# RWKV scan of a two-block network: bonus add, low parts and zero fills taken off POOL, fewer operand parts per stretch

## Chip, cores and metric

One core of a Trainium2 chip. The metric is the device time in microseconds of one launch, the median of several runs. One further execution was taken with the hardware profiler; all rows below come from it.

## What is computed

The reference runs a first block (two layers of attention, gated linear attention and pooling) and a second block whose stages are an SGU, an RWKV mixer, a latent attention and another SGU. Only the RWKV stage is touched by the change. It has 1024 model channels, 16 heads of 64 and 768 tokens (512 and 256 of context), and scans the tokens in both directions:

```
xs   = h + center_shift(h) * mu                      # six mixes: r, k, v, z, decay, a
rkvz = einsum(xs[:4], w_in)                          # four projections 1024x1024
decay, a = lora(xs[4]), lora(xs[5])                  # low rank, per direction
S    = S * w_t - s_kk x (kk_t * a_t) + v_t x k_t     # state 64x64, per head and direction
y_t  = S r_t
yn   = layernorm_per_head(y) * ln_gain + ln_bias
bonus = sum(r * k_dir * r_k) * v
out  = ((yn + bonus) * silu(z)) @ w_out
```

Everything is float32. Large matmuls are done as three products of high and low parts (x = hi + lo, each rounded for TensorE).

## The kernel before, in words

The RWKV stage is the class `Rwkv`. It has two halves, and in both TensorE's instructions keep the order in which the Python code issues them, while the order on the other engines is set by a scheduler when the program is built. Each engine then works through its own queue in order, POOL (GpSimd) and SP (DMA issue) too.

**Features** (`features`, L1316). `strips` runs the projections k, r, z, v: 32 strips of 48 matmuls, in stretches of 12; 1536 matmuls per side product. In between, side generators get credits per stretch: `lora`, `operands` at the rate `OPS`, `by_tokens` (values transposed to tokens) at 2.5 and `first` at 3.0. `operands` (L1570) makes, for each of eight slices of 128 channels (two heads), what the scan needs, in some 15 parts: low-rank matmuls (L1603) with ACT's tanh (L1604), a head norm (transposes, L1264), then for each direction a running sum on VectorE (L1625), exponentials on ACT, and the products L1619, L1646, L1647 and L1649 on VectorE that fill the tiles `st_ar` and `st_bk`. These go to DRAM, and `within` (L1679) multiplies them in blocks of a chunk of 64 tokens; its results go to DRAM as well (`rw_md`, `rw_mo`). `first` starts when the projection z is done: it runs `inverse` 0 on VectorE and `merge` 0, waits until all eight slices have their operands, opens the scan's pool, and starts `inverse` 1 on POOL and the first products.

**Inverse and merge.** `inverse` (L1802) inverts 96 triangular blocks of 32x32 by 31 pairs of a product (L1819) and a subtraction (L1821), and writes the result to DRAM (L1825, then two DMAs). `merge` loads it into a tile `TT`, fills the upper blocks with zeros (L1846, POOL) and joins two 32x32 inverses into one of 64x64 by small matmuls (L1854, L1866). `TT` is a new tile for each slice.

**Scan** (`scan`, L1689). For p = 0 to 8, `lanes` walks 12 steps of slice p and of slice p − 1, interleaved: a step is a chain of 64x64 matmuls on TensorE (all L1885) and copies between (rh L1892, VU L1897 on ACT and L1898, state L1908, SV L1914 and L1915). `weave` mixes in the products of coming slices, `merge` of slice p + 1, `inverse` of slice p + 2 on POOL, and `output` of slice p − 2. `output` normalizes `yacc` (L1945, ACT's square L1948, L1955), scales it on ACT (L1957), adds the bonus on POOL (L1959), multiplies with z on VectorE (L1961), splits into high and low part (`split`, L174, low part on POOL at L178), and multiplies by w_out, whose low weight parts come from VectorE and every third from POOL (`wtile`, L141).

Of the kernel before, what the change touches and what calls it, by code (L numbers as in the profile page):

```python
# [16 lines left out]
ALU = mybir.AluOpType  # L17
# [334 lines left out]
class Block1:  # L352
# [353 lines left out]
    def gla(self, l, P, ap, tmp, idxT, qb, kb, vb, rb, mix_tile):  # L706
# [21 lines left out]

        def merge(X, Y, mask, first):
            pps = [net.aux() for h in range(4)]  # L730
            for c in range(NCH):
                for h in range(4):
                    nc.tensor.matmul(pps[h][:, c * 128:c * 128 + 128], lhsT=X[h * 32:h * 32 + 32, c * 128:c * 128 + 128],
                                     rhs=Y[h * 32:h * 32 + 32, c * 128:c * 128 + 128], start=True, stop=True,
# [9 lines left out]
        for m in (64, 32, 16, 8, 4, 2, 1):  # L744
# [11 lines left out]
            if m == 64:  # L756
                merge(X, X, self.lev64f, True)
            else:
# [358 lines left out]
CH = 64  # L1117
NS = (S + C) // CH
# [31 lines left out]
def chain(*gens):  # L1150
    for g in gens:
        yield from g
# [29 lines left out]
OW = (0.0, 0.4, 1.0)  # L1182
BANKS = (4, 4)
PACE = 0.4
OPS = 2.4
WT = 3


class Rwkv:
# [32 lines left out]
    def work(self, tag, shape, bufs, k=0):  # L1222

        at = {"T12": 1, "TT": (3, 2, 0)[k % 3]}.get(tag)
        if at is None:
            return (self.op if tag[:3] == "inv" and tag != "invW" else self.ap).tile(shape, F32, tag=tag, name=tag, bufs=bufs)
        return shaped(self.big(at), shape)
# [86 lines left out]
    def features(self):  # L1314
# [22 lines left out]
        with tc.tile_pool(name="rws", reuse_waits="tile", bufs=9) as self.xsp:  # L1337
# [3 lines left out]
            vt = chain(*[self.by_tokens(f) for f in range(KD)])  # L1341
            sides = [(self.lora(), 1.0), (ops, OPS), (vt, 2.5), (self.first(), 3.0)]
            self.sides = ops, vt
# [131 lines left out]
    def first(self):  # L1475

        tc = self.net.tc
        while self.done["xs"] != "v":
            yield
        self.cur = cur = [{} for k in range(KD)]  # L1480
        X = [self.big(2), self.big(3)]
        cut = lambda t, a, n: t[:, a:a + n]
        place = {"invA": [cut(X[0], 0, 1024)], "invT": [cut(X[1], 0, 1024)], "invP": [cut(X[0], 1024, 256)]}
        turn = {}

        def work(tag, shape, bufs, k=0):
            if tag == "T12":
                return self.work(tag, shape, bufs, k)
            turn[tag] = turn.get(tag, -1) + 1
            return shaped(place[tag][turn[tag] % len(place[tag])], shape)  # L1490

        acc = self.net.aux
        for _ in self.inverse(0, cur[0], work, self.net.nc.vector):
            yield
        t = self.big(2)
        place = {"invW": [cut(t, 768, 256), cut(t, 1024, 256)], "TT": [self.big(3)]}
        yield from self.merge(0, cur[0], work, acc)

        while self.done["op"] < KD:
            yield  # L1500
        self.right.close()
        self.op = self.right.enter_context(tc.tile_pool(name="rwc", reuse_waits="tile", bufs=1, side="right"))
        self.masks(self.op.tile([128, 2, 64], F32, name="rmask"))
        self.slot, self.groups, self.gs = 0, 0, []
        self.steps_to_come = self.ahead(cur)
        inv = self.inverse(1, cur[1], self.work, self.net.nc.gpsimd)
        for _ in range(9):
            next(self.steps_to_come)
            for _ in range(2):
                next(inv)  # L1510
                yield
        yield from inv
# [319 lines left out]
    def merge(self, k, cur, work, acc):  # L1832

        net, nc, ap = self.net, self.net.nc, self.ap
        mt = cur["mt"]
        TA = cur["TT"] = work("TT", [128, 2, NS, CH], 1, k)
        T12 = work("T12", [128, 2, 24, 32], 1)
        T1, M = T12[:, 0], T12[:, 1]
        TF = TA.rearrange("p d s t -> p (d s) t")
        for e in range(2):  # L1840
            nc.sync.dma_start(M[64 * e:64 * e + 32], self.mo[k][e])
            nc.sync.dma_start(T1[64 * e:64 * e + 32], self.blocks(mt[1], e, 0))
            for h in range(2):
                q = 64 * e + 32 * h
                nc.sync.dma_start(TF[q:q + 32, :, 32 * h:32 * h + 32], self.blocks(mt[0], e, h))
            nc.gpsimd.memset(TF[64 * e + 32:64 * e + 64, :, 0:32], 0.0)  # L1846
        for _ in range(8):
            yield
        for g in range(3):
            pw = acc()  # L1850
            for x in range(8):
                for e in range(2):
                    a, bq = slice(64 * e, 64 * e + 32), slice(64 * e + 32, 64 * e + 64)
                    nc.tensor.matmul(pw[bq, x * 32:x * 32 + 32], lhsT=M[a, g * 8 + x, :], rhs=T1[a, g * 8 + x, :],  # L1854
                                     start=True, stop=True, tile_position=(64 * e, 64 * e + 32))
            yield
            W = work("invW", [128, 8, 32], 2)
            for e in range(2):
                bq = slice(64 * e + 32, 64 * e + 64)
                nc.scalar.copy(W[bq].rearrange("p a b -> p (a b)"), pw[bq, :256])  # L1860
            yield
            pz = acc()
            for x in range(8):
                for e in range(2):
                    a, bq = slice(64 * e, 64 * e + 32), slice(64 * e + 32, 64 * e + 64)
                    nc.tensor.matmul(pz[a, x * 32:x * 32 + 32], lhsT=W[bq, x, :], rhs=TF[bq, g * 8 + x, 32:64],  # L1866
                                     start=True, stop=True, tile_position=(64 * e + 32, 64 * e))
            yield
            for e in range(2):
                a = slice(64 * e, 64 * e + 32)  # L1870
                nc.scalar.activation(TF[a, g * 8:g * 8 + 8, 32:64], pz[a, :256].rearrange("p (x c) -> p x c", c=32), AF.Copy, scale=-1.0)
            yield
# [60 lines left out]
    def output(self, k, cur):  # L1933

        net, nc, ap, P = self.net, self.net.nc, self.ap, self.P
        T = S + C
        rows = slice(k * 128, k * 128 + 128)
        col = lambda t, j: t[:, j:j + 1]
        y = cur["y"]
# [11 lines left out]
        z, bonus = (ap.tile([128, T], F32, tag="f", name="ld_" + n) for n in "zb")  # L1951
# [4 lines left out]
        yield  # L1956
        nc.scalar.activation(y, y, AF.Identity, scale=col(P["lg"], k), bias=col(P["lb"], k))  # L1957
        yield
        nc.gpsimd.tensor_tensor(y, y, bonus, ALU.add)  # L1959
        yield  # L1960
        nc.vector.scalar_tensor_tensor(y, y, 0.5, z, ALU.mult, ALU.mult)  # L1961
        yield
        yh = ap.tile([128, T], F32R, tag="yh", name="yh", bufs=1)
        yl = ap.tile([128, T], F32R, tag="yl", name="yl", bufs=1)
        net.split(yh, yl, y, nc.gpsimd)
        yield
        for f in range(KD):
            if f % 4 == 0:
                hi, lo = net.wtile([(0, net.I["rwkv_w_out_2"][0][rows, f * 128:f * 128 + 512])], 1, 512)
            a, b = net.acc(), net.acc()  # L1970
            outs = [(a, 0, S), (b[:, :C], S, T)]
            net.strip(outs, [(hi[:, 0], lo[:, 0])], [(yh, yl)], c0=f % 4 * 128)
            yield
            self.b2.residual(self.i, f, outs, ap if k == KD - 1 else None)
# [488 lines left out]
```

## Time and profile before

| | us |
|---|---|
| median of 3 runs | 4227.73 |
| lowest, highest | 4226.45, 4228.69 |
| the profiled execution's own time | 4218.81 |
| its span | 4216.9 |
| RWKV features, about | 2009 to 2532 |
| eight operand slices in them | 2140 to 2393 |
| RWKV scan, about | 2536 to 3072 |

Times in rows are microseconds from the start of the span unless marked ns. PE is TensorE, PEld its weight loads, DVE VectorE, ACT ScalarE, POOL GpSimd, SP the engine that issues DMAs. A releaser ("[1.2 <-ACT tmp L1604]") is what ended the idle time in front of an instruction. PEclk is the clock that TensorE was granted, as a share of full speed.

### The profile page before, as it was taken

The page shows a single profiled execution, that of the slowest core. Times are in us where ns is not written, and L with a number is a line of the kernel's source. Part 1 is how long each engine was busy: PE and PEld are TensorE (multiplying, and loading weights), DVE is VectorE, ACT ScalarE, POOL GpSimd, SP SyncE. Part 2 cuts the span into 40 slices and gives each one's busy share as a digit, 9 for nine tenths or more (in the row PEclk, how much of TensorE's full clock was granted, in tenths as well). Part 3 has the DMA queues.
Part 4 walks back from the last instruction along what each step waited for, and adds up shares of the span by engine and source line. Part 5 has one row for each costly group of instructions (what it writes and reads, how often), then busy time and mean ns, then how long its engine had stood idle before and what let it go on. Part 6 is the DMA issues. An engine that isn't in the chain of part 4 may idle for free. (4 is left out here: it accounts for less than half of the span.)

```text
span 4216.9 us, 67232 instructions
## 1 busy us (share of the span) xinstructions
PE 3855.6 (91%) x26432; PEld 3192.2 (76%) x26432; DVE 2461.7 (58%) x4804; ACT 1545.2 (37%) x2945; POOL 1317.8 (31%) x1340
## 2 busy tenths in 40 slices
PE   8999999999999999998887797588789899998999
PEld 7867777787877788887766576477577788887887
DVE  7836445865554434444767644477643778883544
ACT  4243223334332422223454433244343455553222
POOL 3321111322111211113445578820121344442221
PEclk9999999999999999999899898799889999999999
DMA  3125543213364322222257866355223121221332
GB/s 92 51 79 162 175 132 90 61 56 100 103 202 158 102 65 61 60 61 78 70 158 202 226 166 156 91 128 124 79 61 114 51 61 52 61 77 62 93 91 85
DMA packets 599015, 431.72 MB, mean 102 GB/s; under 512 B 193436, under 2 KB 532140, under 8 KB 598700
## 3 DMA queue, kind: packets, MB, share of 16 engines
q1 hardware_dynamic: 593756, 414.97, 34.1%
q0 software_dynamic: 4944, 12.46, 1.2%
q8 instruction: 209, 3.42, 0.3%
q14 instruction: 106, 0.87, 0.1%
HBM read 354.46 MB, written 68.68 MB: 100 GB/s over the span
## 5 line engine op out<-in xcount | busy, mean ns | idle before, releaser
L138 ACT CAST whi<-wraw 128x1024 fp32r<-128x1024 f32 (+3 forms) x471 | 457.5, 972 | 1183.0 <-PE acc L160 971.4
L141 POOL TENSOR_TENSOR wlo<-wraw,whi 128x1024 fp32r<-128x1024 f32 (+2 forms) x205 | 426.9, 2083 | 1291.3 <-ACT whi L138 1182.1
L160 PE MATMUL acc<-hh,whi 128*128 128x512 f32 (+2 forms) x1776 | 625.2, 377 | 9.5 <-ACT hh L421 5.0
L160 PE MATMUL acc<-hl,whi 128*128 128x512 f32 (+2 forms) x1776 | 620.8, 374 | 2.5 <-DVE hl L422 2.5
L160 PE MATMUL acc<-hh,wlo 128*128 128x512 f32 (+2 forms) x1776 | 620.3, 374 | 2.0 <-DVE wlo L141 2.0
L141 DVE TENSOR_TENSOR wlo<-wraw,whi 128x1024 fp32r<-128x1024 f32 (+3 forms) x266 | 330.6, 1244 | 467.1 <-ACT whi L138 420.7
L160 PEld LDWEIGHTS acc<-hh,whi 128*128 128x128 f32 (+1 forms) x1776 | 314.7, 188 | 84.0 <-ACT whi L138 17.3
L160 PEld LDWEIGHTS acc<-hh,wlo 128*128 128x128 f32 (+1 forms) x1776 | 314.4, 187 | 63.4 <-DVE wlo L141 2.8
L160 PEld LDWEIGHTS acc<-hl,whi 128*128 128x128 f32 (+1 forms) x1776 | 314.6, 188 | 62.3 <-DVE hl L422 4.1
L160 PE MATMUL acc<-wlo,hh 128*128 128x256 f32 (+1 forms) x896 | 297.2, 332 | 6.5 <-DVE wlo L141 6.5
L160 PE MATMUL acc<-whi,hh 128*128 128x256 f32 (+1 forms) x896 | 298.1, 335 | 2.9 <-ACT hh L978 2.3
L160 PE MATMUL acc<-whi,hl 128*128 128x256 f32 (+1 forms) x896 | 293.4, 331 | 1.5 <-DVE hl L979 1.5
L999 DVE SCALAR_TENSOR_TENSOR xT<-acc,mod,xT 128x512 f32<-128x512 f32 x256 | 185.6, 746 | 139.6 <-PE acc L160 138.9
L160 PEld LDWEIGHTS acc<-wlo,hh 128*128 128x128 f32 x896 | 179.5, 201 | 20.4 <-DVE wlo L141 7.3
L160 PEld LDWEIGHTS acc<-whi,hh 128*128 128x128 f32 x896 | 179.4, 201 | 20.5 <-ACT hh L978 2.9
L160 PEld LDWEIGHTS acc<-whi,hl 128*128 128x128 f32 x896 | 178.4, 200 | 16.3 <-DVE hl L979 2.4
L160 PE MATMUL wide<-xsh,whi 128*128 128x512 f32 (+1 forms) x512 | 147.4, 371 | 16.5 <-ACT xsh L1384 16.5
L160 PE MATMUL wide<-xsl,whi 128*128 128x512 f32 (+1 forms) x512 | 142.0, 360 | 17.0 <-POOL xsl L1385 13.5
L160 PE MATMUL wide<-xsh,wlo 128*128 128x512 f32 (+1 forms) x512 | 140.0, 356 | 0.0
L160 PE MATMUL acc<-ffgh,whi 128*128 128x512 f32 x352 | 139.9, 400 | 0.0
L160 PE MATMUL acc<-ffgl,whi 128*128 128x512 f32 x352 | 138.4, 395 | 0.0
L160 PE MATMUL acc<-ffgh,wlo 128*128 128x512 f32 x352 | 138.3, 395 | 0.0
(625 smaller groups left out, 8754.9 us busy)
## 6 DMA issues: line engine op xcount, KB each, us to landing
ada_w<-in_ada_w SPq DMA_DIRECT2D x32, 1536.0 KB
wraw<-in_sgu_w_in SPq DMA_DIRECT2D x96, 512.0 KB
wraw<-in_w_up SPq DMA_DIRECT2D x88, 512.0 KB
wraw<-in_w_in SPq DMA_DIRECT2D x44, 512.0 KB
wraw<-in_w_down SPq DMA_DIRECT2D x32, 512.0 KB
wraw<-in_sgu_w_out SPq DMA_DIRECT2D x32, 512.0 KB
wraw<-in_rwkv_w_in SPq DMA_DIRECT2D x32, 512.0 KB
bk<-rw_bk SPq DMA_DIRECT2D x24, 512.0 KB
```

The source lines that it names most:

```text
L138: nc.scalar.copy(hi, raw)
L141: eng.tensor_tensor(lo, raw, hi.bitcast(F32), ALU.subtract)
L160: mm(out, lhsT=a, rhs=b[:, t0:t1], start=first and n == 0, stop=last and n == 2)
L999: nc.vector.scalar_tensor_tensor(dst[k], ps, m[:, 16 + k, j:j + 1], dst[k], ALU.mult, ALU.add)
```

## The change

Four edits, all in the RWKV stage:

- `OPS`, the parts of `operands` issued per stretch of 12 projection matmuls, goes from 2.4 to 1.7.
- The bonus add (L1959) and the low part of `yacc` (L178) are done by VectorE.
- The low parts of w_out's weights are all done by VectorE.
- The tile `TT` of a merge is allocated for slices 0, 1 and 2 alone and then used in turn, so that its zeros, now written by VectorE, are written for these three only. The other parts of the tile are written anew by every merge.

```diff
@@ -1182,7 +1182,7 @@
 OW = (0.0, 0.4, 1.0)
 BANKS = (4, 4)
 PACE = 0.4
-OPS = 2.4
+OPS = 1.7
 WT = 3
 
 
@@ -1478,6 +1478,7 @@
         while self.done["xs"] != "v":
             yield
         self.cur = cur = [{} for k in range(KD)]
+        self.tts = []
         X = [self.big(2), self.big(3)]
         cut = lambda t, a, n: t[:, a:a + n]
         place = {"invA": [cut(X[0], 0, 1024)], "invT": [cut(X[1], 0, 1024)], "invP": [cut(X[0], 1024, 256)]}
@@ -1833,7 +1834,10 @@
 
         net, nc, ap = self.net, self.net.nc, self.ap
         mt = cur["mt"]
-        TA = cur["TT"] = work("TT", [128, 2, NS, CH], 1, k)
+
+        if k < 3:
+            self.tts.append(work("TT", [128, 2, NS, CH], 1, k))
+        TA = cur["TT"] = self.tts[k % 3]
         T12 = work("T12", [128, 2, 24, 32], 1)
         T1, M = T12[:, 0], T12[:, 1]
         TF = TA.rearrange("p d s t -> p (d s) t")
@@ -1843,7 +1847,8 @@
             for h in range(2):
                 q = 64 * e + 32 * h
                 nc.sync.dma_start(TF[q:q + 32, :, 32 * h:32 * h + 32], self.blocks(mt[0], e, h))
-            nc.gpsimd.memset(TF[64 * e + 32:64 * e + 64, :, 0:32], 0.0)
+            if k < 3:
+                nc.vector.memset(TF[64 * e + 32:64 * e + 64, :, 0:32], 0.0)
         for _ in range(8):
             yield
         for g in range(3):
@@ -1956,17 +1961,17 @@
         yield
         nc.scalar.activation(y, y, AF.Identity, scale=col(P["lg"], k), bias=col(P["lb"], k))
         yield
-        nc.gpsimd.tensor_tensor(y, y, bonus, ALU.add)
+        nc.vector.tensor_tensor(y, y, bonus, ALU.add)
         yield
         nc.vector.scalar_tensor_tensor(y, y, 0.5, z, ALU.mult, ALU.mult)
         yield
         yh = ap.tile([128, T], F32R, tag="yh", name="yh", bufs=1)
         yl = ap.tile([128, T], F32R, tag="yl", name="yl", bufs=1)
-        net.split(yh, yl, y, nc.gpsimd)
+        net.split(yh, yl, y)
         yield
         for f in range(KD):
             if f % 4 == 0:
-                hi, lo = net.wtile([(0, net.I["rwkv_w_out_2"][0][rows, f * 128:f * 128 + 512])], 1, 512)
+                hi, lo = net.wtile([(0, net.I["rwkv_w_out_2"][0][rows, f * 128:f * 128 + 512])], 1, 512, nc_lo=nc.vector)
             a, b = net.acc(), net.acc()
             outs = [(a, 0, S), (b[:, :C], S, T)]
             net.strip(outs, [(hi[:, 0], lo[:, 0])], [(yh, yl)], c0=f % 4 * 128)
```

Line numbers of the changed kernel are higher by one to five in this part of the file (L1679 is L1680, L1885 is L1890, L1959 is L1964).

TensorE in the features, at the second operand slice: the two block products (`st_ar`, `st_bk`) of a slice and the low-rank matmuls and transposes of the next; left out are the projection matmuls between. Before:

```order
L1679 MATMUL aux<-st_ar,st_bk 64x64 x24
...
L1679 MATMUL aux<-st_ar,st_bk 64x64 x24
L1603 MATMUL aux<-hw,w_17814 128x512 x2
L1603 MATMUL aux<-hw,w_17814 128x256 x2
...
L1603 MATMUL aux<-ha,a_17815 128x512 x2
L1603 MATMUL aux<-ha,a_17815 128x256 x2
L1264 MATMUL aux<-ident,hs_rep 128x128 x6
...
L1679 MATMUL aux<-st_ar,st_bk 64x64 x24
```

In the change, at the same slice:

```order
L1680 MATMUL aux<-st_ar,st_bk 64x64 x24
...
L1680 MATMUL aux<-st_ar,st_bk 64x64 x24
...
L1604 MATMUL aux<-hw,w_17891 128x512 x2
L1604 MATMUL aux<-hw,w_17891 128x256 x2
L1604 MATMUL aux<-ha,a_17892 128x512 x2
L1604 MATMUL aux<-ha,a_17892 128x256 x2
L1264 MATMUL aux<-ident,hs_rep 128x128 x6
...
L1680 MATMUL aux<-st_ar,st_bk 64x64 x24
```

Before, the marks "..." stand for 24, 12 and 36 projection matmuls; in the change for 36, 12 and 60. Over all, the eight slices lie between the 444th and the 1080th of the 1536 projection matmuls before, and between the 444th and the 1380th in the change; merge 0 is at the 1356th in both.

VectorE in the last part of the features, during inverse 0 (its two tiles are the xx tiles). Before:

```order
L1821 TENSOR_TENSOR xx_19673<-xx_19673,xx_19672 96x8x24
L1819 TENSOR_TENSOR xx_19672<-xx_19672,xx_19673 96x175
L1821 TENSOR_TENSOR xx_19673<-xx_19673,xx_19672 96x7x25
L1819 TENSOR_TENSOR xx_19672<-xx_19672,xx_19673 96x156
L1565 TENSOR_TENSOR rst<-aux,rst 128x512
```

In the change:

```order
L1820 TENSOR_TENSOR xx_19350<-xx_19350,xx_19351 96x135
L1611 SCALAR_TENSOR_TENSOR kq<-ld_k,col_rwkv,aux 128x512
L1611 SCALAR_TENSOR_TENSOR kq<-ld_k,col_rwkv,aux 128x256
L1822 TENSOR_TENSOR xx_19351<-xx_19351,xx_19350 96x27x5
L1620 SCALAR_TENSOR_TENSOR tmp<-tmp,kq 128x768
L1650 TENSOR_TENSOR st_ar<-eb,kq 128x12x64
L1820 TENSOR_TENSOR xx_19350<-xx_19350,xx_19351 96x156
L1620 SCALAR_TENSOR_TENSOR tmp<-tmp,kq 128x768
L1648 SCALAR_TENSOR_TENSOR st_bk<-tmp 128x12x64
```

The operands of the last slices now stand between the steps of the inverse, which had its place among the projection's work alone.

POOL in the scan before, at output 0: the end of one inverse, the zero fill of a merge, and further down the bonus add in the middle of the next inverse:

```order
L1825 TENSOR_SCALAR invA<-invT 96x1024
L1829 DMA rw_mt<-invT 96x1024
L1819 TENSOR_TENSOR invP<-invA,invT 96x31
L1828 DMA rw_mt<-invA 96x1024
L1821 TENSOR_TENSOR invT<-invT,invP 96x31
L1846 MEMSET xx_22597 32x24x32 x2
...
L1819 TENSOR_TENSOR invP<-invA,invT 96x240
L1959 TENSOR_TENSOR yacc<-yacc,ld_b 128x768
L1821 TENSOR_TENSOR invT<-invT,invP 96x12x20
```

VectorE in the change, at the same output 0:

```order
L1960 TENSOR_TENSOR yacc<-yacc,acc 128x512
L1960 TENSOR_TENSOR yacc<-yacc,acc 128x256
L1903 COPY VU<-aux 64x2x64
L1964 TENSOR_TENSOR yacc<-yacc,ld_b 128x768
L1903 COPY VU<-aux 64x2x64
L1913 SCALAR_TENSOR_TENSOR st<-st,rw_ec,aux 128x64 x2
L1966 SCALAR_TENSOR_TENSOR yacc<-yacc,ld_z 128x768
L1920 TENSOR_TENSOR SV<-st,rw_ec 64x2x64
L1913 SCALAR_TENSOR_TENSOR st<-st,rw_ec,aux 128x64 x2
L1920 TENSOR_TENSOR SV<-st,rw_ec 64x2x64
L178 TENSOR_TENSOR yl<-yacc,yh 128x768
```

The add and the low part (yl) stand among the copies and state updates of the lanes. In POOL's queue of the change the inverses follow one another with no memset of a merge and no operation of an output between.

## Rows read from the trace of the kernel before

**Rows 1.** The page, part 1: busy time, share and instructions of each engine.
```profile
PE 3855.6 (91%) x26432; PEld 3192.2 (76%) x26432; DVE 2461.7 (58%) x4804; ACT 1545.2 (37%) x2945; POOL 1317.8 (31%) x1340
```

**Rows 2.** Stretches: from, to, length, busy (instructions) per engine, PEclk, DMA share, GB/s.
```profile
core 0: us, PE busy (x) PEld busy (x) DVE busy (x) ACT busy (x) POOL busy (x), PEclk, DMA share, GB/s
2140.00:2393.00 253.00, 192.47 (x1572) 154.31 (x1572) 181.70 (x147) 132.82 (x201) 133.35 (x76) 0.91 0.74 202
2393.00:2479.00 86.00, 70.86 (x364) 58.47 (x358) 60.23 (x89) 24.27 (x34) 56.52 (x80) 0.86 0.71 194
...
2650.00:2695.00 45.00, 0.76 (x14) 0.50 (x10) 1.84 (x4) 0.79 (x4) 39.52 (x72) 0.53 0.20 50
2695.00:2710.00 15.00, 14.05 (x162) 11.55 (x162) 9.09 (x30) 3.62 (x11) 13.34 (x24) 0.70 0.03 7
2710.00:3042.00 332.00, 289.31 (x4981) 237.33 (x4976) 241.78 (x765) 130.53 (x400) 71.06 (x93) 0.95 0.48 115
```

**Rows 3.** Timeline of TensorE in the scan: start, duration, operation, [idle before, releaser].
```profile
2695.30 1.12 PE L1885 MATMUL aux<-rh,xx 64*64 64x64 f32 x16 [44.29 <-DVE rh L1892]
```

**Rows 4.** Timeline of VectorE at the same place.
```profile
2693.61 1.43 DVE L1961 SCALAR_TENSOR_TENSOR yacc<-yacc,ld_z 128x768 f32<-128x768 f32 x1 [43.12 <-POOL yacc L1959]
```

**Rows 5.** Timeline of POOL at the same place.
```profile
2691.78 1.80 POOL L1959 TENSOR_TENSOR yacc<-yacc,ld_b 128x768 f32<-128x768 f32 x1
```

**Rows 6.** Timeline of ScalarE, the operation before the bonus add.
```profile
2647.00 1.03 ACT L1957 ACTIVATE yacc<-yacc,col_rwkv 128x768 f32<-128x768 f32 x1 [0.25 <-DVE yacc L1955]
```

**Rows 7.** Waits of POOL, 2535 to 3075: total, times, longest.
```profile
POOL yacc L1959 <- ACT yacc L1957: 131.7, 6, 47.7
POOL xx L1846 <- PE aux L1885: 74.8, 3, 30.4
```

**Rows 8.** Waits of TensorE, 2140 to 2393.
```profile
PE aux L1679 <- DVE st_bk L1647: 40.6, 13, 5.6
PE aux L1264 <- ACT tmp L1604: 15.9, 11, 3.7
PE aux L1603 <- ACT tmp L1604: 4.0, 5, 2.4
```

**Rows 9.** Timeline of TensorE between two slices: projection matmuls and one `within`.
```profile
2319.25 0.51 PE L160 MATMUL wide<-xsl,whi 128*128 128x512 f32 x2
2319.60 0.52 PE L160 MATMUL wide<-xsh,wlo 128*128 128x512 f32 x2
...
2332.88 2.82 PE L1679 MATMUL aux<-st_ar,st_bk 64*64 64x64 f32 x48 [4.57 <-DVE st_bk L1647]
```

**Rows 10.** Groups of VectorE's instructions, 2710 to 3042: busy us, mean ns, idle before.
```profile
L1915 DVE TENSOR_TENSOR SV<-st,rw_ec 64x128 f32<-64x128 f32 x65 | 24.3, 394 | 1.5
...
L1961 DVE SCALAR_TENSOR_TENSOR yacc<-yacc,ld_z 128x768 f32<-128x768 f32 x6 | 5.7, 953 | 4.5 <-POOL yacc L1959 4.5
```

**Rows 11.** Groups of POOL's instructions, 2536 to 3075.
```profile
L1959 POOL TENSOR_TENSOR yacc<-yacc,ld_b 128x768 f32<-128x768 f32 x8 | 14.5, 1809 | 131.7 <-ACT yacc L1957 131.7
```

**Rows 12.** Timeline of VectorE at 2575 us.
```profile
2575.52 1.85 DVE L1915 TENSOR_TENSOR SV<-st,rw_ec 64x128 f32<-64x128 f32 x1
```

**Rows 13.** Timeline of POOL at 2575 us.
```profile
2575.29 1.94 POOL L1825 TENSOR_SCALAR invA<-invT 96x1024 f32<-96x1024 f32 x1
```

**Rows 14.** Groups of VectorE's instructions, 2140 to 2393: first and last of five.
```profile
L1625 DVE TENSOR_TENSOR_SCAN tmp<-rreset,tmp 128x768 f32<-128x768 bf16 x16 | 28.8, 1843 | 34.8 <-ACT tmp L1621 34.8
...
L1646 DVE TENSOR_TENSOR st_ar<-eb,ld_r 128x768 f32<-128x768 f32 x16 | 22.0, 1373 | 11.4 <-PE aux L1679 5.0 <-DMA ld_r<-rw_r 4.0 <-ACT kd L1617 1.2
```

**Rows 15.** Groups of VectorE's instructions, 2390 to 2540: inverse 0.
```profile
L1821 DVE TENSOR_TENSOR xx<-xx,xx 96x31 f32<-96x31 f32 (+15 forms) x31 | 17.9, 578 | 1.0
L1819 DVE TENSOR_TENSOR xx<-xx,xx 96x31 f32<-96x31 f32 (+15 forms) x31 | 17.4, 563 | 1.0
```

**Rows 16.** Timeline of POOL: the first product of inverse 1.
```profile
2413.47 0.62 POOL L1819 TENSOR_TENSOR invP<-invA,invT 96x31 f32<-96x31 f32 x1
```

**Rows 17.** Line L1825, the end of an inverse, 2400 to 2800: min/median/max ns, first and last start.
```profile
L1825 POOL TENSOR_SCALAR invA<-invT x7: 1912/1944/2059, 2480.9 to 2751.7; 96x1024 f32<-96x1024 f32 x7
```

**Rows 18.** Line L1854, a merge's matmuls in the scan, 2400 to 2800.
```profile
L1854 PE MATMUL acc<-xx x384: 191/191/257, 2571.3 to 2785.2; 32*32 32x32 f32 x192
```

## The prediction

> **What bounds the kernel now.** I read the page's busy shares first, then the stretches of the RWKV stage, then in each stretch the wait that ends last. TensorE is busy 91% of the span and no other engine passes 58% [rows 1], so time can come only from places where TensorE stands still or runs at its lower clock. Only the RWKV stage (about 2009 to 3072 us) is touched. Two stretches of it stand out [rows 2]. From 2650 to 2695 TensorE is busy 0.76 us of 45, and in the 15 us behind that its granted clock is 0.70. From 2140 to 2393, where the eight operand slices run among the projection matmuls, it is busy 192.5 of 253 us, so 60.5 us stand still. Behind these the projections' last part (2393 to 2479) shows 15 us of standing still, and the rest of the scan (2710 to 3042) 43 us of 332.
>
> The long hole has one cause. TensorE waits 44.29 us for VectorE's rh copy [rows 3]; VectorE waited 43.12 us in front of its L1961 [rows 4] for POOL's bonus add L1959, which started at 2691.78 [rows 5]. What that add needs had been there since 2648.03: ACT's L1957 began at 2647.00 and took 1.03 us [rows 6]. So the add stood 43.7 us in POOL's program order behind inverse work. POOL's order shows it: from the memsets (L1846) on nearly a whole inverse stands between them and the add. POOL's other waits are of the same make: 74.8 us in front of the memsets for TensorE's readers and 131.7 us in front of the bonus adds for ACT [rows 7]. Since POOL serves scan operations and inverses in one queue, each of the two holds the other up.
>
> In the operands the waits are TensorE's: 40.6 us at `within` (L1679) for VectorE's st_bk, 15.9 and 4.0 us for ACT's tanh [rows 8], together all of the 60.5. They are the latency of one slice's chain, ACT to VectorE to TensorE, and they appear where few projection matmuls stand between two links: the L1679 at 2332.88 waited 4.57 us [rows 9] with 24 of them ahead of it.
>
> **The change, part by part.**
>
> *Bonus add, low part and memsets leave POOL.* The hole of 44.3 us goes. What is late next there is ACT's L1957 and two VectorE operations, all done within some 4 us of 2648, where the lanes have other work: I take −44.3. Bounds: −44.3, and −20 if a second wait of half the length forms. The clock behind the hole comes back as well: 14.05 busy us at 0.70 [rows 2] would be 9.8 at full clock, −4.2 (bounds 0 and −4.2).
>
> VectorE pays for it. An add of 128x768 is 0.95 us there (its L1961 [rows 10]) against 1.81 on POOL [rows 11]. Eight bonus adds and eight low parts are 15.2 us; five low parts of w_out weights (128x512) and six memsets are no wider, so under 0.95 each; at 0.7, an estimate, they are 7.7. VectorE gets 23 us more. It is busy 241.8 of 332 us in the scan [rows 2], so the bounds are 0 and +23. The order of VectorE puts each bonus add between the two VU copies of a lane, on the chain of a step, and the low part behind SV: one operation of the two per head pair on the path, 8 x 0.95 = +7.6. At the end, where the last output has no lanes beside it, bonus and low part are each 0.86 shorter: −1.7. The scan in sum: −44.3 − 4.2 + 7.6 − 1.7 = −42.6.
>
> Does VectorE lose more than that beside POOL's inverses? One row says that it can: an L1915 of VectorE took 1.85 us from 2575.52 [rows 12], where it takes 0.39 on average [rows 10], and POOL's L1825 ran from 2575.29 to 2577.23 [rows 13], ending with it. I bound the added cost by 0 and by 1.46 (1.85 − 0.39) for each of ten added operations that run while inverses last (five outputs, two each): +15. I take 0, since the other operations of an inverse are a third as long (72 in 39.5 us, 0.55 each [rows 2]). The Trainium skill (SBUF — State Buffer, "Who interferes with whom") has a rule for this: a VectorE operation with two inputs in SBUF and a GpSimd operation that reads SBUF exclude each other for a whole instruction. The row agrees with it; by that rule each of the ten would wait up to one POOL operation of 0.55 us, 5.5 in all, and the forecast would be 4161 in place of 4155.
>
> *Zeros kept in three tiles.* It takes all eight pairs of memsets from POOL (three now run on VectorE, five are gone) and their wait for TensorE of 74.8 us [rows 7]. POOL was ahead of the scan there, so nothing on the path changes; POOL's own schedule gets shorter, which counts in the slow rival below. The first memset is now on VectorE, ahead of two operand operations in the last part of the features; the bound is 0 to +5, taken inside the next item.
>
> *Operands at 1.7 parts per stretch.* TensorE's order shows a slice among some 117 projection matmuls in place of 79.5; all eight end after 1380 of 1536 in place of 1080. Two projection matmuls take 0.35 us (starts at 2319.25 and 2319.60 [rows 9]), 0.174 each. A slice now takes 253/8 = 31.6 us with 24.1 busy [rows 2]. With 37.5 more matmuls (6.5 us) it is 30.6 of work in a chain of 31.6. Waits will not vanish wholly, since the links are uneven (12 to 60 matmuls apart): I take 3 us of waiting a slice, 24 in all against 60.5, −36. Bounds: −56 (1 us of waiting left in each slice) and 0 (the chain stretches as far as the matmuls do).
>
> The work moved comes out of the last part, where it was cover. VectorE's operand operations are five groups of 22.0 to 28.8 us for eight slices [rows 14], some 127, with the small ones 18 a slice. VectorE's order now has two slices between first and last operation of inverse 0, which took 17.9 + 17.4 = 35.3 us alone [rows 15]. To that come 25 us of projection work (the 60.2 that VectorE is busy in the stretch [rows 2], less the inverse): 36 + 35 + 25 = 96 us on VectorE, where TensorE has its 70.9 and two slices' own work, 2 x (24.1 − 79.5 x 0.174) = 20.6, so 91.5. VectorE stood still 26 of the 86 us, since its operations wait for TensorE and ACT in turn; if that stays, the stretch takes 122 us, in which TensorE idles 30 in place of 15: +15. Bounds: −15 (no idle time left) and +35 (the operands' chains lie end to end with the inverse).
>
> The clock: 192.5 busy us at a mean of 0.91 and 70.9 at 0.86 [rows 2] hold 17 and 10 us that full clock would give back; with fewer holes I take a third, −9 (bounds 0 and −20). Features in sum: −36 + 15 − 9 = −30.
>
> *Inverse 1 starts later.* It waits for the last operand slice, whose `within` ran at 2393, 139 us ahead of the features' end E (2532); with 156 projection matmuls and the transposes behind it, it is now some 48 us ahead of E. Before, POOL had the inverse's first product at 2413.5 [rows 16], 20 us behind it. On POOL the last operation of an inverse, L1825, is at 2480.9 (E − 51) for the first of seven and at 2751.7 for the last [rows 17]: 45 apart. Now it begins at about E − 28 and ends at E + 10 to 20. Merge 1 wants it at 2571.3 [rows 18], E + 39; merge 2 at about E + 81, later ones every 54 us. Cost nothing, with 10 to 20 us to spare; if that is gone, see the slow rival.
>
> The sum is −42.6 − 30 = −72.6 against the profiled execution's own 4218.8: 4146. That execution is 8.9 us under the median of the runs, so I say **4155** for the median of 4227.7.
>
> **Rivals.**
> 1. *The features give nothing.* The chain of a slice is VectorE's and stretches with the matmuls, or VectorE binds the last part by its full bound. For: VectorE is busy 182 of 253 us in the operands already [rows 2]. Against: TensorE's waits are short and many, as latency makes them. Only the scan's part stays, with some of the VectorE cost: −43 + 5 = −38, 4190. Chance 0.22.
> 2. *The features give all.* Waits go to 1 us a slice and merge 0 is not waited for: −43 − 56 + 0 = −99, with the clock's −9 it is −108: 4120 to 4129. For: the 60.5 us are all named waits. Against: the count of VectorE's work above. Chance 0.17.
> 3. *The hole is halved, not gone.* VectorE in its own order waits at the bonus add for ACT or for the load of the bonus, with the lanes' copies behind it. For: the order gives it a fixed place. Against: L1957 was done long before. −18 in place of −42.6, with the features' −30 it is −48: 4180. Chance 0.09.
> 4. *Slower: inverses bind the scan.* POOL's inverses come 45 us apart [rows 17], the first merges 42 apart, so if inverse 1 ends later than about E + 30, merge 2 waits, and every us beyond moves the whole scan. To eat up 73 us it must end at E + 103, and to be slower by 0.2% at E + 112: it would have to start over 60 us behind the features' end. That needs a queue (SP's loads of the inverse behind waiting ones, or the pool's release) that I don't see: a start 20 us after the last `within` is what the trace has. Chance 0.05, 4240.
> 5. *It doesn't do what it says.* Something else of the scan stays in POOL's queue between inverses and holds VectorE as the add did. POOL's order of the change has inverses and nothing of an output at that place. Chance 0.02, 4228.
>
> **How the numbers follow.** The forecast has 0.45, at 4155 with a range of its own of 4134 to 4180. The range of 4116 to 4200 takes in rivals 1, 2 and 3 and the +15 of the two engines' meeting; it leaves out rivals 4 and 5 and the tails, some 0.15. A measurement of this kernel tells about 0.2% (8.5 us) from no change. Faster by more: 0.45 + 0.22 + 0.17 + 0.09 = 0.93; within it 0.02; slower 0.05.
>
> **What would show it.** Right: no wait of over 5 us at L1961 or rh in the scan, a granted clock of 0.95 or more all through it, TensorE's waits in the operands at 20 to 30 us, a wait of some 20 us near merge 0 that ends with VectorE, and inverse 1 on POOL ending 10 to 20 us behind the features. Wrong: as much idle TensorE in the features as before (rival 1), merges that wait for POOL (rival 4), or a long VectorE wait for ACT or a load at the bonus add (rival 3).

## The result and the profile after

| | before | after |
|---|---|---|
| median (4 runs each) | 4227.09 us | 4158.01 us |
| lowest to highest | 4221.69 to 4228.69 | 4156.49 to 4160.44 |
| ratio, 95% interval | | 0.9839 (0.9822 to 0.9856) |
| profiled execution, span | 4216.9 | 4155.1 |
| first projection matmul to first lane matmul (features) | 2010.0 to 2539.5: 529.5 | 2011.8 to 2518.2: 506.4 |
| first lane matmul to the last group of them (scan) | 2539.5 to 3038.0: 498.5 | 2518.2 to 2981.0: 462.8 |

The kernel is 69 us faster by the medians, against 4155 forecast and a range of 4116 to 4200. The two profiled executions differ by 62 us: 23 in the features, 36 in the scan and the rest in front of and behind these. That the medians differ by 69 is partly chance, as the profiled execution of before was some 8 us below its median and that of after 1 us.

The page of the kernel after, part 1 (to be held against [rows 1]):

```profile
PE 3858.5 (93%) x26432; PEld 3195.4 (77%) x26432; DVE 2461.6 (59%) x4831; ACT 1543.5 (37%) x2945; POOL 1271.3 (31%) x1303
```

TensorE does as much work as before, in a shorter span. The stretches, with the columns of [rows 2]: most of the operands' slices, the piece up to merge 0 (in which the last slice runs on, to 2459), the rest of the features, the scan.

```profile
2143.00:2398.00 255.00, 218.22 (x1554) 174.01 (x1554) 185.72 (x165) 130.90 (x195) 129.41 (x71) 0.90 0.73 202
2398.00:2445.00 47.00, 37.91 (x280) 29.68 (x278) 41.58 (x72) 24.44 (x38) 17.62 (x9) 0.96 0.84 227
2445.00:2518.00 73.00, 66.82 (x622) 55.66 (x622) 14.75 (x25) 20.89 (x42) 44.67 (x81) 0.91 0.74 197
2518.00:2981.00 463.00, 386.69 (x6690) 323.54 (x6692) 320.42 (x997) 172.84 (x540) 225.71 (x409) 0.89 0.55 129
```

In the first of these TensorE stands still 36.8 us of 255, where it was 60.5 of 253 for nearly as many matmuls (1554 and 1572). Its waits in the features (2100 to 2540), largest first:

```profile
PE aux L1264 <- ACT tmp L1605: 16.4, 12, 3.9
PE aux L1680 <- DVE st_bk L1648: 8.2, 4, 3.5
PE wide L160 <- POOL xsl L1385: 6.1, 7, 1.3
PE aux L1604 <- ACT tmp L1681: 4.1, 1, 4.1
```

The wait for st_bk has fallen from 40.6 to 8.2 [rows 8]; that for ACT's tanh is where it was, 16.4 in place of 15.9. In the scan the hole of [rows 3] is gone, and this is what is left (TensorE's waits, 2495 to 3015):

```profile
PE aux L1890 <- DVE VU L1903: 25.9, 30, 1.9
PE aux L1890 <- DVE rh L1897: 20.1, 13, 12.9
PE acc L1775 <- DMA G<-rw_ar: 9.2, 6, 6.3
```

G is a tile of a product in the scan, loaded from `rw_ar`. The longest wait, 12.9 us, is new in its size. VectorE stands in front of a low part of w_out's weights, and the copy rh that TensorE waits for stands behind it in VectorE's queue. VectorE's timeline there, and the first bonus add:

```profile
2533.06 0.33 DVE L1933 TENSOR_TENSOR yacc<-yacc,aux 128x64 f32<-128x64 f32 x2
2545.76 0.98 DVE L141 TENSOR_TENSOR wlo<-wraw,whi 128x512 fp32r<-128x512 f32 x1 [12.36 <-ACT whi L138]
...
2630.78 0.96 DVE L1964 TENSOR_TENSOR yacc<-yacc,ld_b 128x768 f32<-128x768 f32 x1 [0.83 <-ACT yacc L1962]
```

The bonus add runs 0.83 us after VectorE came to it. The load of those weights was later than before because of SP's queue: behind the first group's loads it now has the merge's loads (L1846, L1849), most of them of the inverse's result. SP's timeline:

```profile
2522.40 1.24 SPq L1758 DMA_DIRECT2D G<-rw_ar  x2
...
2530.56 1.20 SPq L1846 DMA_DIRECT2D xx<-rw_mt  x2
2531.80 1.66 SPq L1758 DMA_DIRECT2D G<-rw_ar  x1
2533.56 2.82 SPq L1849 DMA_DIRECT2D xx<-rw_mt  x4
...
2542.37 4.76 SPq L135 DMA_DIRECT2D wraw<-in_rwkv_w_out  x2
```

The same place in the kernel before, SP and VectorE:

```profile
2546.99 1.23 SPq L1757 DMA_DIRECT2D G<-rw_ar  x2
...
2561.36 4.72 SPq L135 DMA_DIRECT2D wraw<-in_rwkv_w_out  x2
...
2564.72 0.98 DVE L141 TENSOR_TENSOR wlo<-wraw,whi 128x512 fp32r<-128x512 f32 x1 [6.97 <-ACT whi L138]
```

From the first G to the weights SP took 14.4 us before and takes 20.0 now; the merge's loads between are 4.0 of the 5.6.

The inverses on POOL, by their last operation (min/median/max ns, first and last start): it began at 2514.9 for the first. The prediction's E, the end of the projections, is 2532 before and 2511 here, so this is 4 us behind E, where I had 10 to 20:

```profile
L1826 POOL TENSOR_SCALAR invA<-invT x7: 1937/1982/2049, 2514.9 to 2777.2; 96x1024 f32<-96x1024 f32 x7
```

### The profile page after: what moved, and what is told of

Read it like the earlier page. It is cut to its first block, busy times and chain, and to the rows that moved or that the text cites. A ratio compares the mean times of both kernels' runs of the same rounds, so it can differ in the third digit from the quotient of the medians.

```text
span 4155.1 us, 67171 instructions
## 1 busy us (share of the span) xinstructions
PE 3858.5 (93%) x26432; PEld 3195.4 (77%) x26432; DVE 2461.6 (59%) x4831; ACT 1543.5 (37%) x2945; POOL 1271.3 (31%) x1303
## 5 line engine op out<-in xcount | busy, mean ns | idle before, releaser
L138 ACT CAST whi<-wraw 128x1024 fp32r<-128x1024 f32 (+3 forms) x471 | 457.4, 971 | 1187.8 <-PE acc L160 972.3
```

The lines of the kernel that those rows point to most:

```text
L138: nc.scalar.copy(hi, raw)
```

## Experiments

Each was timed against the kernel before on the same chip; "features" and "scan" are taken from its profiled execution as in the table above. The changed kernel itself was run again with the last three. The time of one and the same kernel scatters by some 0.3% from execution to execution (the change: 4148.9 to 4163.2), and the ratios' intervals are 0.0013 to 0.0022 to either side, so differences under some 8 us between two of these are not told apart. A profile is of one execution, and two profiles of the change differ by 6 us in the scan.

| kernel | median us | ratio (95%) | features | scan |
|---|---|---|---|---|
| the change, first time | 4158.01 | 0.9839 (0.9822 to 0.9856) | 506.4 | 462.8 |
| the change again | 4158.38 | 0.9844 (0.9830 to 0.9857) | 504.8 | 469.3 |
| the rate 1.7 alone | 4201.58 | 0.9956 (0.9940 to 0.9972) | 515.7 | 498.8 |
| all but the rate | 4176.33 | 0.9894 (0.9872 to 0.9915) | 543.1 | 447.0 |
| bonus add back on POOL | 4197.28 | 0.9942 (0.9920 to 0.9964) | 498.4 | 504.9 |
| weights' low parts as before | 4177.14 | 0.9896 (0.9879 to 0.9914) | 509.4 | 483.2 |
| first weights loaded early | 4154.30 | 0.9845 (0.9831 to 0.9860) | 497.2 | 470.3 |
| two more VectorE operations | 4170.40 | 0.9887 (0.9870 to 0.9903) | 506.7 | 483.0 |
| zeros as before | 4164.75 | 0.9873 (0.9859 to 0.9888) | 519.0 | 466.6 |
| the rate at 2.0 | 4165.10 | 0.9874 (0.9859 to 0.9889) | 520.9 | 455.2 |
| merge's loads by ScalarE | 4159.11 | 0.9849 (0.9835 to 0.9863) | 504.7 | 457.4 |
| merge's loads by POOL | 4168.57 | 0.9871 (0.9857 to 0.9885) | 509.8 | 473.0 |
| loads by POOL, weights early | 4165.51 | 0.9862 (0.9847 to 0.9878) | 500.4 | 470.5 |

**The two halves apart.** The kernel before with `OPS = 1.7` and nothing else:

```diff
-OPS = 2.4
+OPS = 1.7
```

> The kernel before with only the operands' rate at 1.7. Theory (the gain has two parts that add: some 25 us in the features from spreading the operands, some 40 us in the scan from POOL's queue): the features shorten by about 23 us as in the change, the wait for the bonus add stays (40 to 55 us, as POOL's inverses start later and the add still stands behind 11 steps of one), so 4195 to 4212 us. Rival A (the rate does nothing by itself): 4227 and features as long as before. Rival B (later inverses on a POOL that also serves the scan make the hole longer): over 4215, with a wait of 65 us or more at the bonus add.

18.6 us less than before (0.0044 x 4217), as expected in time; the features give 13.8 of it (23 expected), and the hole stays, but at 28.3 us it is shorter than the 40 to 55 that I expected. VectorE's timeline:

```profile
2664.88 1.34 DVE L1961 SCALAR_TENSOR_TENSOR yacc<-yacc,ld_z 128x768 f32<-128x768 f32 x1 [28.30 <-POOL yacc L1959]
```

VectorE's waits for the add are 36.2 us in all, 14.5 less than before (50.7), and still the scan is no shorter (498.8 against 498.5). Two other waits have grown by as much: TensorE's for G, 13.6 in place of 5.7, and VectorE's for w_out's weights, 12.6 in place of 7.1. They are the ones that the change has as well:

```profile
PE acc L1774 <- DMA G<-rw_ar: 13.6, 7, 6.4
```

The change with `OPS = 2.4`, so the other three edits alone:

> The change with the operands' rate back at 2.4, so the edits on POOL, VectorE and the zeros alone. Theory: the features are as long as before (about 529 us from the first projection matmul to the scan), the scan as short as in the change (about 463 us between the first and last lane matmul in place of 498), so 4178 to 4190 us. Rival A: about 4160, the rate is worth nothing. Rival B: the scan is shorter still, since inverses start 50 us earlier, 4165 to 4175.

44.7 us less than before (0.0106 x 4217). The time lies between the theory's and rival B's, and both halves of its profile differ from the theory: the scan is 16 us shorter than in the change, which was rival B's point, and the features are 13.6 longer than before. The waits for st_bk, of up to 8.3 us, make 5 of these (45.3 us in place of 40.6); the rest is not traced. The parts add up in time, within the noise: 18.6 + 44.7 = 63 of 66 to 68. Stage by stage they do not. Beside the other edits the rate gives in the features and takes in the scan: 543.1 − 506.4 = 37 and 462.8 − 447.0 = 16 in the profiles, 21 to 23 net by the ratios. The waits say where most of the 16 are. In this kernel's scan:

```profile
PE aux L1890 <- DVE rh L1897: 11.8, 13, 6.4
...
PE acc L1775 <- DMA G<-rw_ar: 1.9, 3, 1.3
```

G is waited for 1.9 us in place of 9.2, and the longest wait at rh is 6.4 in place of 12.9: 7.3 + 6.5 = 13.8 of the 16. Both are waits for loads that SP issues.

**The edits on POOL one by one.** The bonus add back on POOL:

```diff
-        nc.vector.tensor_tensor(y, y, bonus, ALU.add)
+        nc.gpsimd.tensor_tensor(y, y, bonus, ALU.add)
```

> The change with the bonus add alone back on POOL. Theory (the add's place in POOL's queue makes the hole, the zeros and low parts only ride along): a wait of 40 to 55 us at VectorE's multiplication with z returns in one place, 4195 to 4212 us. Rival (the zeros' memsets and the low parts held POOL, and with these gone the add comes in time): under 4170.

41 to 43 us above the change by the ratios: the add by itself makes a hole again, though no memset of a merge and no low part is left on POOL in the scan. The time is as expected, but it is two waits of VectorE now, not one of 40 to 55:

```profile
2658.58 1.36 DVE L1966 SCALAR_TENSOR_TENSOR yacc<-yacc,ld_z 128x768 f32<-128x768 f32 x1 [29.58 <-POOL yacc L1964]
...
2727.47 1.23 DVE L1966 SCALAR_TENSOR_TENSOR yacc<-yacc,ld_z 128x768 f32<-128x768 f32 x1 [8.94 <-POOL yacc L1964]
```

The low parts of w_out's weights as before, every third on POOL:

```diff
-                hi, lo = net.wtile([(0, net.I["rwkv_w_out_2"][0][rows, f * 128:f * 128 + 512])], 1, 512, nc_lo=nc.vector)
+                hi, lo = net.wtile([(0, net.I["rwkv_w_out_2"][0][rows, f * 128:f * 128 + 512])], 1, 512)
```

> The change without the edit on the low parts of w_out's weights (every third on POOL again). Theory: worth nothing, 4154 to 4164 us; the wait of 12.9 us near the start of the scan, where VectorE stands at the first such low part for its weights' load, stays, since that one was VectorE's before as well. Rival A: that wait goes with the edit, 4143 to 4150. Rival B: one low part on POOL stands behind inverses and holds TensorE, over 4170.

0.0052 to 0.0057 above the change, 22 to 24 us: rival B, by a way that I had not seen. VectorE waits at the bonus add, which is its own now, for the bonus to be loaded:

```profile
2714.49 1.09 DVE L1964 TENSOR_TENSOR yacc<-yacc,ld_b 128x768 f32<-128x768 f32 x1 [23.74 <-DMA ld_b<-rw_bonus]
```

That load is issued by SP at 2710.47, directly behind a load of weights, and SP had done nothing from 2682.35 on:

```profile
2679.80 2.55 SPq L1796 DMA_DIRECT2D VU<-rw_vt  x4
2710.06 0.36 SPq L135 DMA_DIRECT2D wraw<-in_rwkv_w_out  x1
2710.47 0.43 SPq L1957 DMA_DIRECT2D ld_b<-rw_bonus  x1
```

What SP waited for is on POOL: the one low part that POOL has up to there, behind an inverse and the first steps of the next. It is the last reader of the weights' only buffer.

```profile
2702.01 0.17 POOL L1814 MEMSET invT<- 96x32 f32 x1
...
2708.77 1.26 POOL L141 TENSOR_TENSOR wlo<-wraw,whi 128x512 fp32r<-128x512 f32 x1
```

POOL ends it at 2710.03, and SP goes on at 2710.06. So POOL's queue holds a buffer, the buffer holds SP's queue, and SP's queue holds VectorE.

The zeros as before, a new tile per merge and POOL's memsets:

```diff
-        if k < 3:
-            self.tts.append(work("TT", [128, 2, NS, CH], 1, k))
-        TA = cur["TT"] = self.tts[k % 3]
+        TA = cur["TT"] = work("TT", [128, 2, NS, CH], 1, k)
...
-            if k < 3:
-                nc.vector.memset(TF[64 * e + 32:64 * e + 64, :, 0:32], 0.0)
+            nc.gpsimd.memset(TF[64 * e + 32:64 * e + 64, :, 0:32], 0.0)
```

> The change with a new tile for every merge again and its zeros written by POOL, as before. Theory of the prediction (POOL is ahead of the scan, the wait for TensorE's readers costs nothing on the path): within 4 us of the change. Rival: POOL stands up to 30 us in front of a memset with an inverse behind it, and since the inverses end later than before, a merge waits for its inverse and the lanes with it: 10 us or more above the change.

0.0029 to 0.0034 above the change in the ratio, 12 to 14 us, not far beyond what can be told apart. The mechanism of the rival did not show: no wait for an inverse, a scan of 466.6 that lies between the change's two. Its profiled execution, slower by 8 us than its median, has the time in the features (519.0 against 505 to 506), where TensorE stands still 77 us in place of 67 to 70. Why is open.

Taken back one at a time, the add, the weights' low parts and the zeros cost some 42 + 23 + 13 = 78 us, though all three together, at the rate 2.4, give 44.7. So their prices do not add: the add or the weights' low parts alone, left in POOL's queue, are enough for a wait of 24 to 30 us. No run has the low part of `yacc` alone back on POOL.

**What VectorE's added work costs.**

```diff
         nc.vector.tensor_tensor(y, y, bonus, ALU.add)
+        for _ in range(2):
+            nc.vector.tensor_tensor(y, y, y, ALU.max)
```

> The change with two further VectorE operations of 128x768 behind each bonus add (the maximum of y with itself, which leaves y as it is): 16 operations, 15.3 us of VectorE, in the chain of the output and among the lanes' copies. Theory of the prediction (about one in two operations of an output lies on the lanes' chain): 6 to 10 us more than the change. Rival A (VectorE has room, nothing on the path): within 3 us. Rival B (all of it on the path, and more beside POOL's inverses): 15 us or more.

0.0043 to 0.0048 more than the change, 18 to 20 us (uncertain by some 9) for 16 operations of 0.95, 15 in all: rival B. The scan's row, and that of the change run again:

```profile
2512.00:2995.00 483.00, 399.65 (x6692) 333.01 (x6691) 337.28 (x1010) 172.47 (x540) 227.80 (x406) 0.86 0.52 123
...
2518.80:2988.00 469.20, 384.75 (x6686) 321.20 (x6688) 321.27 (x996) 172.60 (x540) 228.30 (x412) 0.88 0.55 127
```

TensorE stands still 83.4 us, and in the change's two profiles 76.3 and 84.5: what the operations cost in idle time, 7 or nothing, is not told apart. The same matmuls are busy 399.65 us in place of 386.69 and 384.75, 13 to 15 more, at a mean granted clock of 0.86 in place of 0.89 and 0.88. So most of what these profiles show of the price stands in busy time at the lower clock.

**The rate between the two.** `OPS = 2.0`:

> The change with the operands' rate at 2.0, between 2.4 and 1.7. At 1.7 the features were 35 us shorter than at 2.4 and the scan 16 us longer, since the first inverse ends 33 us later in the profile. Theory (both go evenly with the rate): features 15 to 22 us longer than in the change, scan 6 to 10 us shorter, so 4 to 12 us above the change. Rival A (the loss in the scan is a threshold, met at 2.0 already): the scan as at 2.4, 447 us, and a time equal to the change's or up to 6 us below. Rival B (the features' waits are gone at 2.0 already): 8 us or more below the change.

0.0030 to 0.0035 above the change, 13 to 15 us, where 4 to 12 were expected. In the profiles the features are 14.5 longer and the scan 7.6 shorter, 7 net: both go evenly with the rate, as the theory had it, and the difference between 7 and 13 to 15 is within the noise.

**To get the 16 us back.** The first tile of w_out's weights at the start of the scan:

```diff
             self.ap = ap
+            self.w0 = net.wtile([(0, I["rwkv_w_out_2"][0][0:128, 0:512])], 1, 512, nc_lo=nc.vector)
...
-                hi, lo = net.wtile([(0, net.I["rwkv_w_out_2"][0][rows, f * 128:f * 128 + 512])], 1, 512, nc_lo=nc.vector)
+                hi, lo = self.w0 if k + f == 0 else net.wtile([(0, net.I["rwkv_w_out_2"][0][rows, f * 128:f * 128 + 512])], 1, 512, nc_lo=nc.vector)
```

> The change, with the first tile of w_out's weights loaded at the start of the scan, ahead of the loads of the next products in SP's queue, in place of behind the merge's loads. Theory: VectorE's wait of 12.4 us for it near the start of the scan goes, TensorE's of 12.9 us with it, some 3 us come back as the loads behind are later: 8 to 12 us less than the change, ratio to the kernel before 0.981 to 0.982 where the change has 0.984. Rival (the time is moved on, the products' loads or merge 1 are late next): same as the change within 4 us.

The rival: 0.9845 against 0.9839 and 0.9844. The wait of 12.9 is gone, and G is waited for 27.1 us, where the change's two profiles have 9.2 and 17.5:

```profile
PE acc L1776 <- DMA G<-rw_ar: 27.1, 6, 12.7
```

Then a merge's loads of the inverse's result off SP's queue, on ScalarE and on POOL:

```diff
-            nc.sync.dma_start(T1[64 * e:64 * e + 32], self.blocks(mt[1], e, 0))
+            (nc.scalar if k else nc.sync).dma_start(T1[64 * e:64 * e + 32], self.blocks(mt[1], e, 0))
...
-                nc.sync.dma_start(TF[q:q + 32, :, 32 * h:32 * h + 32], self.blocks(mt[0], e, h))
+                (nc.scalar if k else nc.sync).dma_start(TF[q:q + 32, :, 32 * h:32 * h + 32], self.blocks(mt[0], e, h))
```

> The changed kernel itself, on the same chip as the three that follow. Expected: the ratio to the kernel before of its first measurement, 0.982 to 0.986.

> The change, with a merge's loads of the inverse's result (six of its eight loads, for slices 1 to 7) issued by ScalarE in place of SP. Theory (the scan lost some 15 us to the later inverses since these loads stand in SP's queue ahead of the products' G and of w_out's weights): TensorE's waits for G (9.2 us) and the wait for the first weights (12.9) fall by 8 to 15 us together, the scan is 452 to 457 us long, 0.0015 to 0.0035 less in the ratio. Rival A (ScalarE's queue is on the lanes' chain and waits for the inverse in it): as long as the change or longer. Rival B (the loads' landing, not their issue, is what is late): within 3 us of the change.

On ScalarE the wait for G falls to 3.0 us, from 9.2 and 17.5, so these loads in SP's queue were its cause. The scan is 457.4 in a profile that is 8 us under its median, but the time is that of the change (0.9849 against 0.9844). ScalarE's copies VU now stand behind its loads, and the wait for them has grown from 26 to 35.7. TensorE's waits in its scan, and ScalarE's timeline at the first such load:

```profile
PE aux L1890 <- DVE VU L1903: 35.7, 31, 6.7
PE aux L1890 <- DVE rh L1897: 13.2, 13, 7.2
...
PE acc L1775 <- DMA G<-rw_ar: 3.0, 5, 1.2
...
2524.55 0.35 ACTq L1846 DMA_DIRECT2D xx<-rw_mt  x1
2524.99 0.26 ACT L1902 COPY VU<-aux 64x128 f32<-64x128 f32 x1 [7.37 <-DMA G<-rw_ar]
```

> The same loads issued by POOL, which writes the inverses and so has no wait for them in its own queue. Theory: the same gain as with ScalarE, 8 to 15 us in the scan, 0.0015 to 0.0035 in the ratio, or a little more since POOL is not on the lanes' chain. Rival (POOL waits in front of the loads for the tile's last readers, with an inverse behind them): a merge waits for its inverse, 0 to 20 us longer than the change.

On POOL it is the rival: 0.0027 above the change, 11 us. The loads take POOL's own time (it is busy 254 us in the scan in place of 226, and its last inverse ends 30 us later) and stand among the steps of the next inverse, and one merge waits for them:

```profile
2776.56 0.31 PE L1859 MATMUL acc<-xx 32*32 32x32 f32 x2 [11.83 <-DMA xx<-rw_mt]
```

> The loads issued by POOL, and the first tile of w_out's weights loaded at the start of the scan. By itself the early tile took the wait of 12.9 us away and brought two of 12.7 and 12.3 us for G. Theory (those came from SP's queue being full, which the loads' move relieves): both gains stand, the scan is 442 to 450 us, 12 to 20 us less than the change. Rival: the waits for G stay over 15 us together, 0 to 6 us less than the change.

Both together: the waits for G stay at 6.7 us, but the merges wait for their loads (10.6 and 6.6 us in its profile), and the time is no better than the change's: 0.9862. None of these beats the change.

## Why the prediction came out

The sign, the range and the two causes were right: POOL's queue in the scan and the operands' latency in the features. The sum of −72.6 stands against −62 between the two profiled executions, and that 4155 lies within 3 us of the median is luck: before's profiled execution happened to be 8 us under its median. Term by term it was less good, and errors of both signs cancelled. None of the signs that I had named for a right prediction came out: a wait at rh is 12.9 us (5 at most), the scan's mean clock is 0.89 (0.95 or more), TensorE's waits in the operands are 36.8 us (20 to 30), the longest wait near merge 0 is 4.0 (some 20), and inverse 1 ends 4 us behind E (10 to 20).

- **The hole.** −44.3 was right as a row, and moving the bonus add is what removes it (with the add back, 42 us). That "the clock comes back", −4.2, is not borne out: the scan's mean clock is 0.87 before over 2540 to 3038 and 0.89 and 0.88 in the change's two profiles, but TensorE's busy time for the same matmuls did not fall (383 before, 387 and 385 after).
- **Weights' low parts on VectorE.** This step failed. I priced them at 0.7 us each as a cost to VectorE and did not ask what POOL's low part holds: a buffer, then SP, then the bonus. Without that edit 22 to 24 us of the gain are gone.
- **VectorE's added work.** Mis-sized, as far as the runs show: +7.6 for 16 large operations, by the half of them on the lanes' path. Two more per add cost 18 to 20 us for 16 (uncertain by some 9), more than the half that I had counted. In the change itself this price is not seen by itself, because POOL's 1.81 us per add and its waits went at the same time. Nor did VectorE get 23 us more as a whole: it is busy 2461.6 us with 27 more instructions, 2461.7 before [rows 1], 10 more in the scan and 9 less in the features. The latter goes with the rate (332 us there with the rate alone, 347 with all but the rate, 340 before); why its operations are shorter then is open.
- **Beside POOL's inverses.** I took 0 out of 0 to 15. It is small but there. VectorE's operations of 128x768 up to 2777, while inverses run, and after:

```profile
L178 DVE TENSOR_TENSOR yl<-yacc,yh 128x768 fp32r<-128x768 f32 x3 | 5.0, 1683 | 0.1
L1964 DVE TENSOR_TENSOR yacc<-yacc,ld_b 128x768 f32<-128x768 f32 x3 | 3.4, 1133 | 2.5 <-ACT yacc L1962 2.5
```

```profile
L178 DVE TENSOR_TENSOR yl<-yacc,yh 128x768 fp32r<-128x768 f32 x4 | 3.8, 959 | 0.1
L1964 DVE TENSOR_TENSOR yacc<-yacc,ld_b 128x768 f32<-128x768 f32 x4 | 3.8, 958 | 3.3 <-ACT yacc L1962 3.3
```

  3 x (0.724 + 0.175) = 2.7 us on six operations (three outputs ran beside inverses, not five). Most of it, 1.6 us, is one low part that met the long last operation of an inverse (VectorE, then POOL); the other five lost 0 to 0.3 each:

```profile
2691.70 2.57 DVE L178 TENSOR_TENSOR yl<-yacc,yh 128x768 fp32r<-128x768 f32 x1
...
2691.41 2.05 POOL L1826 TENSOR_SCALAR invA<-invT 96x1024 f32<-96x1024 f32 x1
```

  The rule of the Trainium skill (SBUF — State Buffer, "Who interferes with whom") agrees with it: these operations have two inputs in SBUF and POOL's read SBUF too, and each lost less than the one POOL operation beside it, 2.05 us for the long one and 0.55 on average for the others [rows 2].
- **Operands.** −36 forecast; idle time there went from 60.5 to 36.8, −24. What was left out: only the waits for st_bk depend on how far the links stand apart; those for ACT's tanh (16.4 us) did not move, as the low-rank matmuls still follow each other with 0 to 24 projection matmuls between, and the transposes follow them with none.
- **The last part of the features.** +15 forecast for VectorE with inverse 0 and two slices; it did not come. From the 1080th projection matmul to merge 0, with the columns of [rows 2]:

```profile
2340.00:2445.00 105.00, 85.15 (x586) 68.32 (x584) 91.53 (x122) 52.22 (x79) 55.04 (x28) 0.90 0.77 215
```

  VectorE is busy 91.5 us where I had counted 96, and TensorE 85 where I had 91.5, so the count of the work was nearly right. But VectorE's own idle time did not stay at 26 us as I assumed: it is 13.5, and the stretch takes 105 us in place of 122. From 2398 to the scan TensorE idles 15.3 us, against 18.9 before behind 2393. The clock's −9 did not come either: TensorE is busy 439.4 us in the features after and 438.2 before. In the features' start, ahead of the operands, it idles 14.5 us in place of 11.9. −24 − 4 + 3 + 1 makes −24, the two profiles say −23, where I had −30.
- **Inverse 1 starts later.** "Cost nothing" failed, though the inverse came even sooner than I had it: 16 us in the scan between the rates 2.4 and 1.7. It was not rival 4: no merge waits for its inverse in the change. The inverse's result is loaded through SP, and its loads, now issued after the scan has begun, stand ahead of G and of w_out's weights, whose waits are 13.8 of the 16. That moving these loads frees the wait for G is shown; that it would give the 16 us back is not, since every queue that they were moved to had a wait of its own. I had named SP's queue in rival 4 as a way to a late inverse, and not as a cost to what stands behind its loads.
- **Zeros.** "Nothing on the path" is not borne out by the ratio: 12 to 14 us (uncertain by some 8), without a mechanism that the profile shows.

## What to carry to other kernels

An operation that waits for another engine, placed in the queue of an engine with long independent work, is late by whatever the scheduler put ahead of it; look for such operations by what they hold, buffers included, since the wait may come out two queues further on. Price work added to an engine in a chain of short steps at its whole duration, not at a share of it: here 16 operations of 0.95 us, 15 us in all, cost 18 to 20 (uncertain by some 9). And when a step is moved later, ask in which DMA queue its loads will then stand, and ahead of what.

## Not expected of the hardware

TensorE's clock moves the time of such edits by as much as its idle time does or more, and it does not follow the sum of that idle time. In the scan the change's two profiles stand still 76 and 84 us at a mean granted clock of 0.89 and 0.88, and the matmuls are busy 387 and 385 us. With two more VectorE operations per add it is 83 us at 0.86, busy 400 us; with the zeros as before 74 us at 0.86, busy 392 us:

```profile
2529.60:2996.20 466.60, 392.41 (x6690) 328.67 (x6692) 321.89 (x995) 172.63 (x539) 231.29 (x413) 0.86 0.53 126
```

Of the two levels (1.2 and 2.4 GHz) the lower was thus granted in more of the last two scans. Which waits bring that about is not shown by these runs.
